# A transformer layer's feed-forward product transposed through VectorE and a DRAM scratch instead of on TensorE

## The chip, the cores and the metric

The kernel runs on one core of a Trainium2 chip. The metric is the device time of one launch in microseconds; the number given is the median of several executions. Beside it there is one execution with the hardware profiler on, from which every row below is taken.

## What is computed

One decoder layer on 256 tokens with 1024 features, all in float32. The part around the change is the SwiGLU feed-forward between two normalizations; the attention before it and the gated input after it are not touched.

```python
f = rmsnorm(h, g_ffn[i])
h = h + (jax.nn.silu(f @ w_gate[i]) * (f @ w_up[i])) @ w_down[i]     # D_FF = 2816
u = rmsnorm(h, g_ple[i])
h = h + jax.nn.sigmoid(u @ w_ple_gate[i]) * (p[i] @ w_ple_proj[i])
return rmsnorm(h, g_final)
```

## The kernel before

**Precision.** Each float32 matmul is three matmuls of TensorE's reduced type `F32R` (`mm3`, lines 174 to 177). A weight chunk is loaded as `raw`, ScalarE copies it rounded to `hi` (line 131), VectorE subtracts to get `lo` (line 158), and TensorE sums hi x H, lo x H and hi x L, where H and L are the same two parts of the activations.

**Weights.** They come in chunks of 1024 KB on SP's queue in the order of the table `CHUNKS`. `raw`, `hi` and `lo` have three buffers each; `need` starts loads three chunks ahead. A load waits until the split three chunks earlier has read its buffer; a cast to `hi` waits until TensorE is done with the chunk three earlier.

**Feed-forward.** The 2816 columns go in blocks (`FF_BLOCKS`): five of 512 and one of 256. For each block `b` the gate weights (`j` = 0) and the up weights (`j` = 1) are two chunks each, of four k-slices; for each of the two row tiles `t` (128 tokens) TensorE makes one accumulation group of 24 matmuls, `ff{b}{t}{j}`. Block 5 has gate and up side by side in one group. The order is b, j, t, k. So of a pair of chunks the first is used in the first half of both row tiles' groups, and the second in the second halves; the second one's buffer, taken over from the first of the pair before, comes free late and is wanted soon.

**The product.** When the gate group ends ScalarE takes its silu into `sg`; when the up group ends VectorE multiplies both into `hid` (128 tokens x 512 columns, line 712). The down-projection needs it with the columns on the partitions. `hid_T` (lines 674 to 682) does that one group later: TensorE transposes it in 128x128 squares with the identity into PSUM (`hidt`), ScalarE rounds into `hidH`, VectorE subtracts into `hidL`.

**Down-projection.** Four accumulators (two row tiles x two halves of the 1024 columns) over 22 k-slices, `wd`. The first two k-slices are done accumulator by accumulator, since the last two PSUM buffers are still being read by ScalarE and VectorE for block 5. The last `hid` is transposed after k = 6.

**What sets the order.** TensorE's order is the order of the code. The other engines' order is made by a scheduler from the order of the code, priorities and estimated times; on the chip each engine then works strictly in that order and waits on semaphores. SP issues all the loads, also in order.

Of the kernel before, what the change touches and what calls it, by code (L numbers as in the profile page):

```python
# [8 lines left out]
F32 = mybir.dt.float32  # L9
F32R = mybir.dt.float32r  # L10
BF16 = mybir.dt.bfloat16
I32 = mybir.dt.int32
AF = mybir.ActivationFunctionType
ALU = mybir.AluOpType
AX = mybir.AxisListType

P = 128
D = 1024
# [4 lines left out]
NQ = 512  # L23
# [13 lines left out]
FF_BLOCKS = [(b * NQ, min(NQ, DFF - b * NQ)) for b in range((DFF + NQ - 1) // NQ)]  # L37
# [25 lines left out]
def layer_kernel(  # L63
# [13 lines left out]
    nc = tc.nc  # L77
# [9 lines left out]
    def acc(name):  # L87
        return ps_acc.tile([P, NQ], F32, tag="acc", name=name)

    def aux(name):  # L90
        return ps_aux.tile([P, NQ], F32, tag="aux", name=name)

    chunks, off = [], 0
    for kind, k0, nk, width, _, _ in CHUNKS:
        n = P * nk * width
# [86 lines left out]
    def tsl(t):  # L182
        return slice(t * P, (t + 1) * P)

    def rsqrt(m, n, name):
        y = sm.tile([P, n], F32, tag=f"rs_y{n}", name=f"{name}_y", bufs=6)
        i = sm.tile([P, n], I32, tag=f"rs_i{n}", name=f"{name}_i")
        a = sm.tile([P, n], F32, tag=f"rs_a{n}", name=f"{name}_a")
        h = sm.tile([P, n], F32, tag=f"rs_h{n}", name=f"{name}_h")
        nc.vector.tensor_scalar(i, m.bitcast(I32), 1, None, op0=ALU.arith_shift_right)  # L190
        nc.vector.tensor_scalar(y.bitcast(I32), i, -1.0, float(0x5F3759DF), op0=ALU.mult, op1=ALU.add)
        nc.vector.tensor_scalar(h, m, -0.5, None, op0=ALU.mult)
        for _ in range(3):
            if n == 1:
                nc.vector.scalar_tensor_tensor(a, y, h, y, op0=ALU.mult, op1=ALU.mult)
            else:
                nc.vector.tensor_tensor(a, y, y, op=ALU.mult)
                nc.vector.tensor_tensor(a, a, h, op=ALU.mult)
            nc.vector.scalar_tensor_tensor(y, a, 1.5, y, op0=ALU.add, op1=ALU.mult)
        return y  # L200
# [64 lines left out]
    ident = cst.tile([P, P], F32, tag="ident", name="ident")  # L265
# [5 lines left out]
    with actx:  # L271
        cadd = at.tile([P, 256], F32, tag="cadd", name="cadd")
        init = at.tile([P, 256], F32, tag="init", name="init")
        for tl, fill in ((cadd, BIG), (init, NEG)):
            nc.gpsimd.memset(tl, 0.0)
            nc.gpsimd.affine_select(
                out=tl[:, P:256], in_=tl[:, P:256], pattern=[[-1, P]], compare_op=ALU.is_ge,
# [335 lines left out]
        i = 0  # L613
# [7 lines left out]
    for nm, g in (("ffn", g_ffn), ("ple", g_ple), ("fin", g_fin)):  # L621
        gB[nm] = act.tile([P, D], F32, tag="gB", name=f"gB{nm}", bufs=2)
        nc.sync.dma_start(gB[nm], g.partition_broadcast(P))
    ff = state["ff"] = ctx.enter_context(tc.tile_pool(name="ff", bufs=2))
    hgs = {}

# [34 lines left out]
    def rstd_h(t, name):  # L661
        s1 = sm.tile([P, 1], F32, tag="ss1", name=f"ss_{name}{t}")
        m1 = sm.tile([P, 1], F32, tag="m1", name=f"m_{name}{t}")
        sqt = ff.tile([P, D], BF16, tag="sqt", name=f"sq_{name}{t}", bufs=1)
        nc.scalar.activation(sqt, h[:, t, :], AF.Square, accum_out=s1)
        nc.vector.tensor_scalar(m1, s1, 1.0 / D, EPS, op0=ALU.mult, op1=ALU.add)
        return rsqrt(m1, 1, f"{name}{t}")


    hidH = ff.tile([P, KF, 256], F32R, tag="hidH", name="hidH", bufs=1)  # L670
    hidL = ff.tile([P, KF, 256], F32R, tag="hidL", name="hidL", bufs=1)
    rf = {0: rstd_h(0, "f")}

    def hid_T(b, t, hid, w):
        nb = w // P
        pt = aux(f"hidt{b}{t}")
        for i in range(nb):
            nc.tensor.transpose(pt[:, i * P : (i + 1) * P], hid[:, i * P : (i + 1) * P], ident)  # L678
        pv = pt[:, :w].rearrange("p (b n) -> p b n", b=nb)
        kk = slice(4 * b, 4 * b + nb)  # L680
        nc.scalar.copy(hidH[:, kk, tsl(t)], pv)  # L681
        nc.vector.tensor_tensor(hidL[:, kk, tsl(t)], pv, hidH[:, kk, tsl(t)].bitcast(F32), op=ALU.subtract)  # L682

    pend = []
    for b, (f0, w) in enumerate(FF_BLOCKS):
        pgu = {}
        both = 2 * w <= NQ
        cw = 2 * w if both else w
        for j in range(1 if both else 2):
            for t in range(NT):  # L690
                ps = acc(f"ff{b}{t}{j}")
                for k in range(KD):
                    wH, wL = need(f"f{b}_{j}", k - k % 4)
                    mm3(
                        ps[:, :cw], FH[:, k, tsl(t)], FL[:, k, tsl(t)], wH[:, k % 4, :], wL[:, k % 4, :],
                        k == 0, k == KD - 1,
                    )
                    if (b, j, t) == (0, 0, 0) and k in (4, 7):
                        trn(1, int(k == 7), FH, FL, "f")
                pgu[(j, t)] = ps  # L700
                if b == 0 and (j, t) == (0, 0):
                    rf[1] = rstd_h(1, "f")
                if pend:
                    hid_T(*pend.pop(0))
                if j == 0:
                    sg = ff.tile([P, NQ], F32, tag="sg", name=f"sg{b}{t}", bufs=3)
                    nc.scalar.activation(sg[:, :w], ps[:, :w], AF.Silu, scale=rf[t])  # L707
                    pgu[("s", t)] = sg
                if j == 1 or both:
                    up = ps[:, cw - w : cw]  # L710
                    hid = ff.tile([P, NQ], F32, tag="hid", name=f"hid{b}{t}", bufs=3)
                    nc.vector.scalar_tensor_tensor(  # L712
                        hid[:, :w], up, rf[t], pgu[("s", t)][:, :w], op0=ALU.mult, op1=ALU.mult
                    )
                    pend.append((b, t, hid, w))

    pd = {(t, c): acc(f"wd{t}{c}") for t in range(NT) for c in range(2)}
    TAILK = KF - 4
# [10 lines left out]
    for k in range(2, TAILK):  # L729
        for t in range(NT):  # L730
            for c in range(2):
                wd_mms(k, t, c)
        if k == 6:
            hid_T(*pend.pop(0))
    UH = act.tile([P, KD, 256], F32R, tag="XH", name="UH")
    UL = act.tile([P, KD, 256], F32R, tag="XL", name="UL")
    for t in range(NT):
        for c in range(2):
# [5 lines left out]
            if (t, c) == (1, 0):  # L744
                trn(0, 0, UH, UL, "u")
    ru = {0: rstd_h(0, "u")}


# [10 lines left out]
    def ple_evac(t, f0, w, ps, prev, mid=None):  # L759
        cc = slice(f0, f0 + w)  # L760
        sg = ff.tile([P, NQ], F32, tag="sg", name=f"sgp{t}{f0}", bufs=3)
        nc.scalar.activation(sg[:, :w], ps[:, :w], AF.Sigmoid, scale=ru[t])
        nc.vector.tensor_tensor(sg[:, :w], sg[:, :w], pp[:, t, cc], op=ALU.mult)
        nc.vector.tensor_tensor(h[:, t, cc], h[:, t, cc], sg[:, :w], op=ALU.add)
        sqt = ff.tile([P, NQ], F32, tag="hid", name=f"sq_o{t}{f0}", bufs=3)
        s3 = sm.tile([P, 1], F32, tag="s3", name=f"s3{t}{f0}")
        if prev is None and t == 0:
            nc.scalar.activation(sqt[:, :w], h[:, t, cc], AF.Square, accum_out=s3)
        else:
            nc.vector.tensor_tensor_reduce(  # L770
                sqt[:, :w], h[:, t, cc], h[:, t, cc], 1.0, 0.0 if prev is None else prev, ALU.mult, ALU.add, s3
            )
        if mid:
            mid()
        if t == 0:
            nc.gpsimd.tensor_tensor(h[:, t, cc], h[:, t, cc], gB["fin"][:, cc], op=ALU.mult)
        else:
            nc.vector.tensor_tensor(h[:, t, cc], h[:, t, cc], gB["fin"][:, cc], op=ALU.mult)
        return s3
# [17 lines left out]
    with tc.manual_schedule(engines={mybir.EngineType.PE, mybir.EngineType.Activation, mybir.EngineType.DVE}):  # L797

        m = sm.tile([P, 1], F32, tag="m3", name="m30")
# [39 lines left out]
def _pack(inputs):  # L839
    import numpy as np  # L840

    a = {k: np.asarray(v) for k, v in inputs.items()}

    def rows(w):
        return np.ascontiguousarray(w.reshape(-1, P, w.shape[-1]).transpose(1, 0, 2))

    xT = a["x"][0].T.reshape(KD, P, 256)
    gT = a["g_attn"][0].reshape(KD, P, 1)
    w0 = a["w_in"][0][:, IN_GROUPS[0][0] : IN_GROUPS[0][1]].reshape(KD, P, W0)
    def cols(names, r0, r1, c0, width):  # L850
        names = names if isinstance(names, tuple) else (names,)
        n = width // len(names)
        return np.concatenate([a[name][0][r0:r1, c0 : c0 + n] for name in names], axis=1)

    flat = [rows(cols(name, k0 * P, (k0 + nk) * P, c0, width)).ravel() for _, k0, nk, width, name, c0 in CHUNKS]
    return {
        "xa": np.ascontiguousarray(np.concatenate([gT, xT, w0], axis=2)).ravel(),
        "x": rows(a["x"][0]),
        "pT": rows(np.ascontiguousarray(a["p"][0, 0].T)).reshape(P, -1),
        "w": np.concatenate(flat),  # L860
        "g_k": a["g_idx_k"][0],
        "g_ffn": a["g_ffn"][0],
        "g_ple": a["g_ple"][0],
        "g_fin": a["g_final"],
        "cs": _tables(),
    }
# [23 lines left out]
```

## Time and profile before

| | us |
|---|---|
| median of 3 runs | 335.91 (335.6 to 335.98) |
| the profiled execution | 335.19 |
| its span, first to last instruction | 333.4 |
| TensorE (PE) busy | 324.3, 97% of the span |
| VectorE (DVE) busy | 227.0, 68% |
| ScalarE (ACT) busy | 175.2, 53% |

Of the chain of work that ended last, 81% of the span is TensorE's, 12% VectorE's, 4% ScalarE's. The feed-forward groups run from about 116 to 240 us, the down-projection from 240 to about 306. In a timeline row the first number is the start in us from the span's start, the second the length; for a matmul the end is modelled and overlaps the next one, so that only the distance of starts tells what it costs. Square brackets give how long the engine had been idle and what released it.

### The profile page before, as it was taken

What the parts mean: (1) busy time and instruction counts of PE and PEld (TensorE: products, weight loads), DVE (VectorE), ACT (ScalarE), POOL (GpSimd) and SP (SyncE); (2) the same over time, 40 slices, a digit from 0 to 9 for tenths busy, and PEclk for the clock granted to TensorE, in tenths of its full rate; (3) what the DMA queues carried; (4) which work ended last, traced back from release to release, by engine and by line L of the source; (5) the groups of instructions that cost most, each with busy time, mean ns of one, the idle gap of its engine ahead of it and who ended that gap; (6) DMA issues with size and microseconds to landing.
All of it is one profiled execution on the core that took longest, in us unless ns stands there. A gap on an engine that the chain in (4) does not pass through costs nothing.

```text
span 333.4 us, 4350 instructions
## 1 busy us (share of the span) xinstructions
PE 324.3 (97%) x1637; PEld 264.4 (79%) x1637; DVE 227.0 (68%) x464; ACT 175.2 (53%) x278; POOL 5.6 (2%) x16
## 2 busy tenths in 40 slices
PE   8999999999999999999999999999999999999992
PEld 8888887677677888888888888888878888888891
DVE  4969999999996886634753655367462535379884
ACT  5957355986674574533562455335443424238623
POOL 2001000000000000000000000000000000000110
PEclk9999999999999999999999999999999999999997
DMA  7996938410337076357435634563365555550002
GB/s 267 418 372 241 362 129 323 141 43 2 126 126 255 0 265 229 134 193 253 158 112 237 252 124 143 239 230 132 144 252 178 201 165 213 161 216 3 0 34 94
DMA packets 10389, 59.71 MB, mean 179 GB/s; under 512 B 1280, under 2 KB 1536, under 8 KB 4096
## 3 DMA queue, kind: packets, MB, share of 16 engines
q1 hardware_dynamic: 10224, 59.24, 48.8%
q8 instruction: 13, 0.21, 0.3%
q10 hardware_dynamic: 144, 0.20, 0.2%
q14 instruction: 8, 0.07, 0.1%
HBM read 58.38 MB, written 1.05 MB: 178 GB/s over the span
## 4 chain that ended last, share of the span: by engine, by line
PE 81%; DVE 12%; ACT 4%; issue 1%; ACTq 0%
PE g L312 13%; PE ff L175 12%; PE ff L177 12%; PE ff L176 12%; PE wd L175 6%; PE wd L176 6%; PE wd L177 6%; DVE lo L158 3%; PE pg L177 2%; PE pg L175 2%; PE pg L176 2%; ACT hi L131 2%; PE hidt L678 1%; DVE score L429 1%; DVE m L428 1%
## 5 line engine op out<-in xcount | busy, mean ns | idle before, releaser
L158 DVE TENSOR_TENSOR lo<-raw,hi 128x1024 fp32r<-128x1024 f32 (+1 forms) x99 | 116.5, 1208 | 62.7 <-ACT hi L131 62.6
L131 ACT CAST hi<-raw 128x1024 fp32r<-128x1024 f32 (+1 forms) x99 | 98.5, 1041 | 91.7 <-PE ff L177 42.4
L175 PE MATMUL ff<-hi,FH 128*128 128x512 f32 x176 | 69.6, 396 | 0.0
L177 PE MATMUL ff<-hi,FL 128*128 128x512 f32 x176 | 68.6, 390 | 0.0
L176 PE MATMUL ff<-lo,FH 128*128 128x512 f32 x176 | 68.5, 389 | 0.0
L177 PEld LDWEIGHTS ff<-hi,FL 128*128 128x128 f32 x176 | 33.0, 188 | 7.0
L176 PEld LDWEIGHTS ff<-lo,FH 128*128 128x128 f32 x176 | 33.1, 188 | 6.5
L175 PEld LDWEIGHTS ff<-hi,FH 128*128 128x128 f32 x176 | 33.1, 188 | 6.5
L175 PE MATMUL wd<-hi,hidH 128*128 128x512 f32 x88 | 35.2, 400 | 0.0
L176 PE MATMUL wd<-lo,hidH 128*128 128x512 f32 x88 | 34.9, 397 | 0.0
L177 PE MATMUL wd<-hi,hidL 128*128 128x512 f32 x88 | 34.6, 393 | 0.0
L312 PE MATMUL g<-hi,XH 128*128 128x512 f32 x64 | 25.8, 408 | 0.0
L312 PE MATMUL g<-hi,XL 128*128 128x512 f32 x64 | 24.8, 393 | 0.0
L312 PE MATMUL g<-lo,XH 128*128 128x512 f32 x56 | 21.6, 391 | 0.0
L175 PEld LDWEIGHTS wd<-hi,hidH 128*128 128x128 f32 x88 | 16.5, 188 | 4.2 <-issue 0.3
L177 PEld LDWEIGHTS wd<-hi,hidL 128*128 128x128 f32 x88 | 16.5, 188 | 4.1
L176 PEld LDWEIGHTS wd<-lo,hidH 128*128 128x128 f32 x88 | 16.5, 188 | 3.6
L707 ACT ACTIVATE sg<-ff,f_y 128x512 f32<-128x512 f32 (+1 forms) x12 | 7.8, 649 | 17.3 <-PE ff L177 17.3
L712 DVE SCALAR_TENSOR_TENSOR hid<-ff,f_y,sg 128x512 f32<-128x512 f32 (+1 forms) x12 | 8.4, 703 | 12.1 <-PE ff L177 10.0
L682 DVE TENSOR_TENSOR hidL<-hidt,hidH 128x512 fp32r<-128x512 f32 (+1 forms) x12 | 7.7, 643 | 11.4 <-ACT hidH L681 11.3
L312 PEld LDWEIGHTS g<-hi,XH 128*128 128x128 f32 x64 | 12.0, 188 | 3.0 <-issue 0.7
L312 PEld LDWEIGHTS g<-hi,XL 128*128 128x128 f32 x64 | 12.0, 188 | 2.7
(201 smaller groups left out, 453.7 us busy)
## 6 DMA issues: line engine op xcount, KB each, us to landing
raw<-in_w_dram SPq DMA_DIRECT2D x48, 1024.0 KB, 4.9
a<-in_xa_dram SPq DMA_DIRECT2D x8, 354.5 KB, 5.8
raw_g<-in_w_dram SPq DMA_DIRECT2D x2, 512.0 KB, 7.7
h<-in_x_dram SPq DMA_DIRECT2D x1, 1024.0 KB, 11.2
raw<-in_w_dram SPq DMA_DIRECT2D x2, 256.0 KB, 4.1
raw<-in_w_dram SPq DMA_DIRECT2D x1, 512.0 KB, 8.3
gBffn<-in_g_ffn_dram SPq DMA_DIRECT2D x1, 512.0 KB, 5.9
gBple<-in_g_ple_dram SPq DMA_DIRECT2D x1, 512.0 KB, 5.9
```

Source lines behind the costliest of these rows:

```text
L131: nc.scalar.copy(hi[:, o : o + step], raw[:, o : o + step])
L158: nc.vector.tensor_tensor(lo[:, o:e], raw[:, o:e], hi[:, o:e].bitcast(F32), op=ALU.subtract)
L175: nc.tensor.matmul(ps, aH, wH, start=start, stop=False)
L176: nc.tensor.matmul(ps, aH, wL, start=False, stop=False)
L177: nc.tensor.matmul(ps, aL, wH, start=False, stop=stop)
L312: nc.tensor.matmul(pss[t][:, :width], aT[:, k, tsl(t)], wT, start=k == 0 and n == 0, stop=k == KD - 1 and n == 2,)
L428: nc.vector.max(m8, s[:, :n])
L429: nc.vector.match_replace(s[:, :n], m8, s[:, :n], SENT)
L678: nc.tensor.transpose(pt[:, i * P : (i + 1) * P], hid[:, i * P : (i + 1) * P], ident)
L682: nc.vector.tensor_tensor(hidL[:, kk, tsl(t)], pv, hidH[:, kk, tsl(t)].bitcast(F32), op=ALU.subtract)
L707: nc.scalar.activation(sg[:, :w], ps[:, :w], AF.Silu, scale=rf[t])
L712: nc.vector.scalar_tensor_tensor(hid[:, :w], up, rf[t], pgu[("s", t)][:, :w], op0=ALU.mult, op1=ALU.mult)
```

## The change

`hid_T` goes, and with it every transpose of the product on TensorE. In its place stand three steps. `hid_out`: VectorE transposes `hid` in 32x32 blocks into `hidb`, and one transfer writes that to a scratch tile in DRAM, `hidd`. `hid_in`: four transfers bring it back, each to 32 partitions of `hidt`, in pieces of 128 columns (512 bytes; 256 in block 5). `hid_split`: ScalarE and VectorE make `hidH` and `hidL` as before, now from SBUF. `hid_step` staggers them: at each new product the split of the one two before, the way back of the one before and the way out of the new one are put into the program; two more steps stand in the down-projection after k = 2 and k = 6. The rows of `w_down` are permuted on the host to fit. The squares of `rstd_h` use the `sg` buffers, and `hid` has two buffers instead of three.

```diff
+    def hid_out(b, t, hid, w):
+        tb = ff.tile([P, NQ], F32, tag="hidB", name=f"hidb{b}{t}", bufs=2)
+        nc.vector.transpose(tb[:, :w], hid[:, :w])
+        dr = dram.tile([P, NQ], F32, tag="hidD", name=f"hidd{b}{t}")
+        nc.sync.dma_start(dr[:, :w], tb[:, :w])
+        return b, t, w, dr
+
+    def hid_in(b, t, w, dr):
+        ht = ff.tile([P, NQ], F32, tag="hidt", name=f"hidt{b}{t}", bufs=2)
+        n = w // 4
+        for g in range(4):
+            nc.sync.dma_start(
+                ht[32 * g : 32 * g + 32, :w].rearrange("p (s n) -> p s n", s=4),
+                dr[:, g * n : g * n + n].rearrange("(s j) n -> j s n", s=4),
+            )
+        return b, t, w, ht
+
+    def hid_split(b, t, w, ht):
         nb = w // P
-        pt = aux(f"hidt{b}{t}")
-        for i in range(nb):
-            nc.tensor.transpose(pt[:, i * P : (i + 1) * P], hid[:, i * P : (i + 1) * P], ident)
-        pv = pt[:, :w].rearrange("p (b n) -> p b n", b=nb)
+        pv = ht[:, :w].rearrange("p (s b i) -> p b s i", s=4, b=nb)
         kk = slice(4 * b, 4 * b + nb)
-        nc.scalar.copy(hidH[:, kk, tsl(t)], pv)
-        nc.vector.tensor_tensor(hidL[:, kk, tsl(t)], pv, hidH[:, kk, tsl(t)].bitcast(F32), op=ALU.subtract)
...
+    def hid_step(*new):
+        if hq["in"]:
+            hid_split(*hq["in"].pop(0))
+        if hq["out"]:
+            hq["in"].append(hid_in(*hq["out"].pop(0)))
+        if new:
+            hq["out"].append(hid_out(*new))
...
-                if pend:
-                    hid_T(*pend.pop(0))
...
-                    pend.append((b, t, hid, w))
+                    hid_step(b, t, hid, w)
...
-        if k == 6:
-            hid_T(*pend.pop(0))
+        if k in (2, 6):
+            hid_step()
```

TensorE's order at the turn from block 0 to block 1 (`ff011` is block 0, row tile 1, up; `ff100` block 1, row tile 0, gate), before and then changed:

```order
L175 MATMUL ff011_1475<-hi19_1333,FH_1258 128x512
L176 MATMUL ff011_1475<-lo19_1458,FH_1258 128x512
L177 MATMUL ff011_1475<-hi19_1333,FL_1259 128x512
L678 MATMUL hidt00_1500<-ident_229,hid00_1473 128x128 x4
L175 MATMUL ff100_1509<-hi20_1353,FH_1258 128x512
L176 MATMUL ff100_1509<-lo20_1515,FH_1258 128x512
```

```order
L175 MATMUL ff011_1481<-hi19_1335,FH_1260 128x512
L176 MATMUL ff011_1481<-lo19_1460,FH_1260 128x512
L177 MATMUL ff011_1481<-hi19_1335,FL_1261 128x512
L175 MATMUL ff100_1517<-hi20_1355,FH_1260 128x512
L176 MATMUL ff100_1517<-lo20_1523,FH_1260 128x512
```

The four transposes of the product of block 0, row tile 0, are gone; the groups now stand directly behind each other. The same holds at eleven more places.

ScalarE's order around the products of block 1 (`hidt10`, `hidt11`) and the casts of chunks 26 to 29, of which the odd ones are the second of their pair, before and then changed:

```order
L131 CAST hi26_1609<-raw26_1607 128x1024 x2
L681 CAST hidH_1310<-hidt10_1654 128x4x128
L707 ACTIVATE sg20_1711<-ff200_1663,f0_y_1317 128x512
L681 CAST hidH_1310<-hidt11_1704 128x4x128
L131 CAST hi27_1666<-raw27_1664 128x1024 x2
L131 CAST hi28_1686<-raw28_1684 128x1024 x2
L707 ACTIVATE sg21_1738<-ff210_1713,f1_y_1390 128x512
L131 CAST hi29_1743<-raw29_1741 128x1024 x2
```

```order
L131 CAST hi26_1610<-raw26_1608 128x1024 x2
L700 CAST hidH_1312<-hidt10_1670 128x4x128
L735 ACTIVATE sg20_1720<-ff200_1679,f0_y_1319 128x512
L131 CAST hi27_1682<-raw27_1680 128x1024 x2
L131 CAST hi28_1702<-raw28_1700 128x1024 x2
L735 ACTIVATE sg21_1747<-ff210_1722,f1_y_1392 128x512
L700 CAST hidH_1312<-hidt11_1794 128x4x128
L131 CAST hi29_1752<-raw29_1750 128x1024 x2
```

The copy of row tile 0 keeps its place, ahead of the cast of chunk 27; that of row tile 1 moves three places on, to directly ahead of the cast of chunk 29.

SP's order over the same stretch (`raw` are weight loads, `hidd` the way out to DRAM, `hidt` the four transfers back), before and then changed:

```order
L120 DMA raw28_1684<-in_w_dram 128x2048
L120 DMA raw29_1741<-in_w_dram 128x2048
L120 DMA raw30_1761<-in_w_dram 128x2048
L120 DMA raw31_1818<-in_w_dram 128x2048
```

```order
L682 DMA hidd10_1639<-hidb10_1637 128x512
L689 DMA hidt10_1670<-hidd10_1639 32x4x128 x4
L120 DMA raw28_1700<-in_w_dram 128x2048
L682 DMA hidd11_1677<-hidb11_1675 128x512
L120 DMA raw29_1750<-in_w_dram 128x2048
L689 DMA hidt11_1794<-hidd11_1677 32x4x128 x3
L120 DMA raw30_1770<-in_w_dram 128x2048
L689 DMA hidt11_1794<-hidd11_1677 32x4x128
L120 DMA raw31_1842<-in_w_dram 128x2048
```

Between the loads stand the new transfers; the last of the four for row tile 1 stands behind the load of chunk 30.

## Rows read from the trace of the kernel before

**Rows 1.** Stretch; its length; busy PE, PEld, DVE, ACT, POOL; clock, DMA share, GB/s:
```profile
138.00:225.00 87.00, 87.00 (x401) 72.16 (x400) 46.73 (x47) 38.98 (x46) 0.00 (x0) 1.00 0.53 191
```
**Rows 2.** TensorE's timeline (start, length) at a turn with no transposes:
```profile
154.93 0.39 PE L177 MATMUL ff<-hi,FL 128*128 128x512 f32 x1
...
155.38 0.39 PE L176 MATMUL ff<-lo,FH 128*128 128x512 f32 x1
```
**Rows 3.** TensorE's timeline at a turn with four transposes:
```profile
160.37 0.39 PE L177 MATMUL ff<-hi,FL 128*128 128x512 f32 x1
160.60 0.60 PE L678 MATMUL hidt<-ident,hid 128*128 128x128 f32 x4
160.95 0.48 PE L175 MATMUL ff<-hi,FH 128*128 128x512 f32 x1
161.27 0.39 PE L176 MATMUL ff<-lo,FH 128*128 128x512 f32 x1
```
**Rows 4.** All instructions on the tile hidt: count, shortest, median, longest ns:
```profile
L678 PE MATMUL hidt<-ident,hid x44: 270/271/273, 137.9 to 260.5; 128*128 128x128 f32 x44
```
**Rows 5.** TensorE's timeline at the turn with two transposes:
```profile
240.21 0.39 PE L177 MATMUL ff<-hi,FL 128*128 128x512 f32 x1
...
240.89 0.40 PE L176 MATMUL wd<-lo,hidH 128*128 128x512 f32 x1
```
**Rows 6.** TensorE's timeline where the fourth down-projection accumulator begins:
```profile
244.64 0.40 PE L177 MATMUL wd<-hi,hidL 128*128 128x512 f32 x1
244.96 0.48 PE L175 MATMUL wd<-hi,hidH 128*128 128x512 f32 x1
245.27 0.39 PE L176 MATMUL wd<-lo,hidH 128*128 128x512 f32 x1
```
**Rows 7.** VectorE's timeline, around block 1 and at the turn into the down-projection:
```profile
155.36 0.75 DVE L712 SCALAR_TENSOR_TENSOR hid<-ff,f_y,sg 128x512 f32<-128x512 f32 x1 [2.00 <-PE ff L177]
159.16 2.36 DVE L158 TENSOR_TENSOR lo<-raw,hi 128x1024 fp32r<-128x1024 f32 x2 [3.06 <-ACT hi L131]
161.44 0.74 DVE L712 SCALAR_TENSOR_TENSOR hid<-ff,f_y,sg 128x512 f32<-128x512 f32 x1
162.10 2.35 DVE L158 TENSOR_TENSOR lo<-raw,hi 128x1024 fp32r<-128x1024 f32 x2
164.37 0.68 DVE L682 TENSOR_TENSOR hidL<-hidt,hidH 128x512 fp32r<-128x512 f32 x1
...
241.72 2.36 DVE L158 TENSOR_TENSOR lo<-raw,hi 128x1024 fp32r<-128x1024 f32 x2 [0.36 <-ACT hi L131]
244.00 0.42 DVE L682 TENSOR_TENSOR hidL<-hidt,hidH 128x256 fp32r<-128x256 f32 x1
244.34 0.47 DVE L712 SCALAR_TENSOR_TENSOR hid<-ff,f_y,sg 128x256 f32<-128x256 f32 x1
```
**Rows 8.** ScalarE's timeline, the same stretches:
```profile
158.07 2.01 ACT L131 CAST hi<-raw 128x1024 fp32r<-128x1024 f32 x2 [5.58 <-PE ff L177]
...
162.70 0.57 ACT L681 CAST hidH<-hidt 128x512 fp32r<-128x512 f32 x1
...
169.87 2.01 ACT L131 CAST hi<-raw 128x1024 fp32r<-128x1024 f32 x2 [2.01 <-PE ff L177]
...
180.75 2.01 ACT L131 CAST hi<-raw 128x1024 fp32r<-128x1024 f32 x2 [5.57 <-PE ff L177]
...
240.64 2.00 ACT L131 CAST hi<-raw 128x1024 fp32r<-128x1024 f32 x2 [0.72 <-PE ff L177]
```
**Rows 9.** SP's timeline of DMA issues, four from 161.55, and the third alone:
```profile
161.55 14.85 SPq L120 DMA_DIRECT2D raw<-in_w_dram  x4
...
173.35 0.33 SPq L120 DMA_DIRECT2D raw<-in_w_dram  x1
```
**Rows 10.** DMA issues: count, KB each, median us from issue to landing:
```profile
raw<-in_w_dram SPq DMA_DIRECT2D x48, 1024.0 KB, 4.9
...
out_dram<-h SPq DMA_DIRECT2D x2, 256.0 KB, 3.2
...
gk<-in_g_k_dram SPq DMA_DIRECT2D x1, 32.0 KB, 11.3
```

More of the change, by code (lines that the diff above doesn't have):

```diff
@@ L623, in layer_kernel @@
         nc.sync.dma_start(gB[nm], g.partition_broadcast(P))
+    dram = ctx.enter_context(tc.tile_pool(name="dram", bufs=3, space=bass.MemoryType.DRAM))
     ff = state["ff"] = ctx.enter_context(tc.tile_pool(name="ff", bufs=2))
@@ L663, in rstd_h @@
         m1 = sm.tile([P, 1], F32, tag="m1", name=f"m_{name}{t}")
-        sqt = ff.tile([P, D], BF16, tag="sqt", name=f"sq_{name}{t}", bufs=1)
+        sqt = ff.tile([P, D], BF16, tag="sg", name=f"sq_{name}{t}", bufs=3)
         nc.scalar.activation(sqt, h[:, t, :], AF.Square, accum_out=s1)
@@ L672, in layer_kernel @@
     rf = {0: rstd_h(0, "f")}
-    def hid_T(b, t, hid, w):
+    def hid_out(b, t, hid, w):
[14 more added lines that the diff above has]
+    def hid_split(b, t, w, ht):
         nb = w // P
-        pt = aux(f"hidt{b}{t}")
-        for i in range(nb):
-            nc.tensor.transpose(pt[:, i * P : (i + 1) * P], hid[:, i * P : (i + 1) * P], ident)
-        pv = pt[:, :w].rearrange("p (b n) -> p b n", b=nb)
+        pv = ht[:, :w].rearrange("p (s b i) -> p b s i", s=4, b=nb)
         kk = slice(4 * b, 4 * b + nb)
-        nc.scalar.copy(hidH[:, kk, tsl(t)], pv)
-        nc.vector.tensor_tensor(hidL[:, kk, tsl(t)], pv, hidH[:, kk, tsl(t)].bitcast(F32), op=ALU.subtract)
-    pend = []
+        hH = hidH[:, kk, tsl(t)].rearrange("p b (s i) -> p b s i", s=4)
+        nc.scalar.copy(hH, pv)
+        nc.vector.tensor_tensor(
+            hidL[:, kk, tsl(t)].rearrange("p b (s i) -> p b s i", s=4), pv, hH.bitcast(F32), op=ALU.subtract
+        )
+    hq = {"out": [], "in": []}
+    def hid_step(*new):
[5 more added lines that the diff above has]
+            hq["out"].append(hid_out(*new))
     for b, (f0, w) in enumerate(FF_BLOCKS):
@@ L710, in layer_kernel @@
                     up = ps[:, cw - w : cw]
-                    hid = ff.tile([P, NQ], F32, tag="hid", name=f"hid{b}{t}", bufs=3)
+                    hid = ff.tile([P, NQ], F32, tag="hid", name=f"hid{b}{t}", bufs=2)
                     nc.vector.scalar_tensor_tensor(
@@ L764, in ple_evac @@
         nc.vector.tensor_tensor(h[:, t, cc], h[:, t, cc], sg[:, :w], op=ALU.add)
-        sqt = ff.tile([P, NQ], F32, tag="hid", name=f"sq_o{t}{f0}", bufs=3)
+        sqt = ff.tile([P, NQ], F32, tag="hid", name=f"sq_o{t}{f0}", bufs=2)
         s3 = sm.tile([P, 1], F32, tag="s3", name=f"s3{t}{f0}")
@@ L853, in cols, with down @@
         return np.concatenate([a[name][0][r0:r1, c0 : c0 + n] for name in names], axis=1)
+    def down(m):
+        parts = [m[f0 : f0 + n].reshape(4, n // P, 32, -1).transpose(1, 0, 2, 3).reshape(n, -1) for f0, n in FF_BLOCKS]
+        return np.concatenate(parts, axis=0)[None]
+    a["w_down"] = down(a["w_down"][0])
     flat = [rows(cols(name, k0 * P, (k0 + nk) * P, c0, width)).ravel() for _, k0, nk, width, name, c0 in CHUNKS]
```

## The prediction

> **What bounds the kernel now.** I read the table of stretches first. From 138 to 225 us TensorE is busy for all of 87.00 us, VectorE for 46.73, ScalarE for 38.98, the DMA engines for 0.53 of the time, and the granted clock is 1.00, the 2.4 GHz level [rows 1]. So in the feed-forward stage whatever TensorE issues is time, and the other engines have room for about as much again. Then I read TensorE's own timeline, by starts and not by busy time, because the ends are modelled. At a turn of one accumulation group to the next with nothing between, the start of L177's last matmul and that of the next group's L176 lie 155.38 - 154.93 = 0.45 us apart, two steps of 0.227 [rows 2]. At a turn with four transposes of the product the same two starts lie 161.27 - 160.37 = 0.90 apart [rows 3]. Four transposes thus cost 0.45 us of TensorE's stream, 0.11 each, although a single record lasts 0.27 [rows 4]: that is depth of the pipeline and not occupancy.
>
> **What is removed.** The 44 transposes are ten groups of four and two groups of two (blocks 0 to 4 are 512 wide, block 5 is 256). All ten turns read alike in the timeline: 10 x 0.45 = 4.5 us. The first group of two gives 240.89 - 240.21 = 0.68 against two plain steps of 0.23, so 0.22, and the second (in the down-projection after k = 6) the same [rows 5]. Together 4.95 us.
>
> What is late next? After each turn TensorE goes straight on to matmuls whose weights are already split. One small stall can go as well: L177 at 244.64 is followed by 244.96 and 245.27, steps of 0.32 and 0.31 where 0.23 is the rule, 0.17 us in all [rows 6]. There the fourth down-projection accumulator waits for a PSUM buffer that VectorE's `hid` of block 5, row tile 1, is the last to read (it starts at 244.34 and takes 0.47). Ahead of it VectorE did a `hidL` of 0.42 [rows 7] and the two halves of a weight split, released by a cast that began at 240.64 [rows 8]. In the changed order that `hidL` (block 5, row tile 0) is no longer between the split and `hid`; the product would be ready at about 244.08 + 0.47 = 244.55, before TensorE needs it at 244.64 + 0.23 = 244.87. I take 0.17 for it; bounds 0 and 0.17.
>
> **What is added, and what covers it.** VectorE gets twelve block transposes. No such operation is in the trace; the nearest is `hidL` with 0.68 us for the same 128x512, and the bound above I take as a whole pair of split halves, 2.36 [rows 7]; below, 0. I take 0.7, so 8 us in over 100 us, on an engine that idles 40 us of 87. Its place matters more than its sum: for row tile 0 it stands directly behind `hid`, for row tile 1 between the two halves of the next split.
>
> SP gets 60 transfers. Weight loads are issued four in 14.85 us, in pairs [rows 9], so SP has time to spare; 60 issues at the 0.33 us of a single one are 20 us over the stage, hidden by SP's own waiting. They move 2816 KB out and 2816 KB back. A full block of the feed-forward reads four loads of 1024 KB [rows 10] and would get 1024 KB more, so at equal efficiency the share of 0.53 becomes 0.66. If the 512-byte pieces of the way back moved at a quarter of the rate of the loads (191 GB/s at a share of 0.53, so 360 at full share, 0.73 us for 256 KB and 2.9 at a quarter), a block of 22 us would hold 2 x 3.6 = 7.3 us more, share 0.86. Both bounds stay under 1, and I book nothing.
>
> The real price can only come through waits in order. ScalarE's copy `hidH` now waits for a transfer, and behind it in ScalarE's order stand weight casts; behind its subtraction on VectorE stand weight splits. Only the cast of a group's second chunk is tight. Take the one at 158.07, released by TensorE's last use of the buffer: its split starts at 159.16, the first half is ready at 160.34 [rows 7, 8], and TensorE first wants that half with the fourteenth matmul of the group that starts at 160.95, at 161.27 + 12 x 0.227 = 163.99 [rows 3]. That is 3.6 us of slack, 3.2 once the transposes in between are gone. Such a cast stands behind a copy in seven places: row tile 0 of blocks 0 to 3, row tile 1 of blocks 0 to 2.
>
> Row tile 0: `hid` of block 1 ends at 156.11 [rows 7], the transpose at about 156.8. The next tight cast behind its copy starts at 169.87; two groups of transposes less make that 168.97, and the copy of 0.57 must precede it [rows 8]: 168.4. So the round trip may take 11.6 us without any loss, 14.8 with the slack. Its rows: 256 KB to DRAM took 3.2 us from issue to landing, a whole 1024 KB load 4.9 [rows 10]; together 8.1. As an upper end for the way back I take the worst small load, 32 KB that landed after 11.3 us behind a queue of large ones [rows 10]: 14.5, still inside.
>
> Row tile 1: `hid` ends at 162.18, half a split follows until 163.3, the transpose until 164.0. Out by 167.2. Three of the four transfers back follow at once, but the fourth stands in SP's order behind the next weight load, whose issue falls at 173.35 [rows 9]. Behind that load's 4.9 us it lands near 178.6. The tight cast stands at 180.75 [rows 8], the copy must start at 180.2; both are less by the same 0.9. Margin 1.6, with the slack 4.8. Block 2 has two parts behind a load in the same way. This is the tightest place, and by the rows nothing is lost there.
>
> Weight loads behind a waiting transfer on SP: the load issued at 173.35 lands at 178.25, and its cast stands behind the one that runs from 180.75 to 182.76, so 4.5 us of waiting cost nothing. In the down-projection the buffers turn once in 5.6 us (24 matmuls of 0.23), with three of them, and the two last copies have still wider room: their columns are wanted only at the end of that stage. The other edits (the squares sharing the `sg` buffers, two `hid` buffers for three) add no instruction and their last readers are a whole group old: 0.
>
> **Two rules of the Trainium skill.** The page "VectorE: DVE Perf Modes" (The three transpose paths) gives 390 ns for a 128x128 transpose on TensorE. By it the 44 would be worth an estimated 17.2 us; the trace's spacing says 0.11 us each, and I go by the trace. The same section, and "DMA: Bandwidth & Descriptors" (Rules for kernel authors), call a plain DMA with a rearranged pattern 19 times slower than the transposing one; by it a read-back of 256 KB would be an estimated 13.9 us and the queues would be the bound, time well over 400 us. No run here shows such a transfer yet; its pieces here are whole runs of 512 bytes. It speaks for the slow rival below.
>
> **The sum.** The profiled execution took 335.19 us (span 333.4). Less 4.95, less 0.17: 330.07. It was 0.72 below the median of the runs, 335.91, so for the median 335.91 - 5.12 = 330.8. I predict 330.8, with its own range 330.2 (the copies save a little more) to 331.8 (a few waits of some tenths).
>
> **Rivals.**
> A, partly paid back. The late parts of the read-back in blocks 1 and 2, or the `hid` at the turn into the down-projection (0.3 us of margin, each us late is a us of TensorE), overrun by 1 to 1.5 us each: 332 to 334.5, say 333. For: the margin of 1.6 is the smallest of all. Against: the cast's slack of 3.2 comes on top.
> B, slower: ScalarE in its order waits for the read-back at the seven tight casts. It costs from a round trip of 14.8 us on, and decides the sign when the excess adds up to 5.1 us, at about 16.1 us on the four places of row tile 0. At 18 us it is 4 x 3.2 = 12.8 us, so 335.91 - 5.12 + 12.8 = 343.6. For: no small-piece read-back from DRAM, and no wait of one transfer for another, is in the trace; the loads come in bursts. Against: the rows make 8.1.
> C, no change: the 5 us come back through A in several blocks at once, or TensorE's steps grow by 1% under the added traffic. Against: with the DMA engines at a share of 0.53 the step already is the plain 0.227.
> D, more gained, toward the page's price: each transpose also holds up the matmuls around it beyond the turn. 318.7 by 17.2 us. Against: two transposes cost half of what four cost, 0.22 and 0.45, so nothing fixed hangs on a turn.
>
> **Numbers.** Forecast 0.79, A 0.09, B 0.08, C 0.03, D 0.01. Within 0.2% (0.7 us) is about what a measurement of this kernel can't tell from no change. Faster takes the forecast, A and D: 0.89; same 0.03; slower 0.08. The range reaches from 330.0 to 333.5, forecast and most of A.
>
> **What would show it.** After: no TensorE instruction writes `hidt`; at the turns L177 to the next L176 0.45 us; down-projection about 4.5 us earlier; no TensorE step over 0.4 us between 138 and 300; ScalarE's `hidH` waits for a transfer, but the casts of second chunks still start when TensorE releases the buffer. Round trips near 8 us. Wrong: TensorE waiting for a `lo` or `hi` right behind a `hidH` or `hidL`, or SP's loads landing later than their casts are due.

## The result and the profile after

The changed kernel takes 331.06 us (330.69 to 331.42) against 335.79 before: ratio 0.9859, 95% interval 0.9842 to 0.9876. Predicted were 330.8, range 330.0 to 333.5. The profiled execution has a span of 329.6 us.

The same stretch of the feed-forward, in the table of stretches (length, busy time and instructions of PE, PEld, DVE, ACT, POOL, then clock, DMA share, GB/s):

```profile
138.00:225.00 87.00, 87.00 (x385) 72.09 (x384) 52.62 (x56) 41.08 (x48) 0.00 (x0) 1.00 0.69 242
```

TensorE is as full as in [rows 1], with 385 instructions for 401. VectorE has gone from 46.73 to 52.62 us, the DMA share from 0.53 to 0.69. TensorE's timeline at the turn that [rows 3] showed, from block 1 to block 2:

```profile
160.43 0.39 PE L177 MATMUL ff<-hi,FL 128*128 128x512 f32 x1
160.65 0.39 PE L175 MATMUL ff<-hi,FH 128*128 128x512 f32 x1
160.88 0.39 PE L176 MATMUL ff<-lo,FH 128*128 128x512 f32 x1
```

L177 to L176 is now 0.45 us, as in [rows 2], where it was 0.90. From the first matmul of the feed-forward to the first of the gate after the down-projection (`pg`) TensorE's timeline of before has

```profile
115.18 0.40 PE L175 MATMUL ff<-hi,FH 128*128 128x512 f32 x1
...
303.53 0.40 PE L175 MATMUL pg<-hi,UH 128*128 128x512 f32 x1
```

that is 303.53 - 115.18 = 188.35 us, and the timeline of the changed kernel

```profile
116.16 0.40 PE L175 MATMUL ff<-hi,FH 128*128 128x512 f32 x1
...
299.44 0.40 PE L175 MATMUL pg<-hi,UH 128*128 128x512 f32 x1
```

that is 183.28: 5.07 less, where the prediction's sum had 4.95 and 0.17, together 5.12. But the stretch begins 0.98 us later than in the profile of before, so that the spans differ by 3.8 only. That part of the program is unchanged; the experiments come back to it.

The new instructions, from the views of the tiles `hidb` and `hidt` (shortest, median, longest ns; first and last start) and of the DMA issues (count, KB each, median us to landing):

```profile
L680 DVE STREAM_TRANSPOSE hidb<-hid x12: 445/706/712, 134.4 to 241.0; 128x512 f32<-128x512 f32 x10, 128x256 f32<-128x256 f32 x2
```
```profile
L689 SPq DMA_DIRECT2D hidt<-hidd x48: 303/430/676, 137.3 to 247.0; - x48
```
```profile
raw<-in_w_dram SPq DMA_DIRECT2D x48, 1024.0 KB, 5.1
...
hidd<-hidb SPq DMA_DIRECT2D x10, 256.0 KB, 2.8
hidt<-hidd SPq DMA_DIRECT2D x40, 64.0 KB, 4.2
```

The block transpose takes 0.71 us, close to the `hidL` of [rows 7]. An issue of the way back holds SP for 0.43 us in the median, not the 0.33 of [rows 9]: the first of the four takes 0.33 or less where SP stood before it, like a load, and the three directly behind another issue mostly take 0.42 to 0.43. The weight loads land in 5.1 us, before in 4.9 [rows 10].

SP's timeline around the products of block 1, where `hidd` is the way out and `hidt` the way back:

```profile
156.94 0.33 SPq L682 DMA_DIRECT2D hidd<-hidb  x1
160.22 1.75 SPq L689 DMA_DIRECT2D hidt<-hidd  x4
162.07 0.38 SPq L120 DMA_DIRECT2D raw<-in_w_dram  x1
164.02 0.34 SPq L682 DMA_DIRECT2D hidd<-hidb  x1
165.13 0.33 SPq L120 DMA_DIRECT2D raw<-in_w_dram  x1
167.86 1.27 SPq L689 DMA_DIRECT2D hidt<-hidd  x3
172.49 0.35 SPq L120 DMA_DIRECT2D raw<-in_w_dram  x1
172.88 0.43 SPq L689 DMA_DIRECT2D hidt<-hidd  x1
```

and ScalarE's timeline, in which these copies stand, with block 2 (square brackets: idle time before it and its releaser):

```profile
163.57 0.62 ACT L700 CAST hidH<-hidt 128x512 fp32r<-128x512 f32 x1 [0.70 <-DMA hidt<-hidd]
...
177.78 0.62 ACT L700 CAST hidH<-hidt 128x512 fp32r<-128x512 f32 x1 [3.46 <-DMA hidt<-hidd]
179.89 2.01 ACT L131 CAST hi<-raw 128x1024 fp32r<-128x1024 f32 x2 [1.49 <-PE ff L177]
...
200.14 0.62 ACT L700 CAST hidH<-hidt 128x512 fp32r<-128x512 f32 x1 [4.07 <-DMA hidt<-hidd]
201.65 2.01 ACT L131 CAST hi<-raw 128x1024 fp32r<-128x1024 f32 x2 [0.89 <-PE ff L177]
```

Row tile 0 of block 1: 163.57 - 156.94 = 6.6 us from the issue of the way out to the copy. Row tile 1: the fourth transfer is issued at 172.88 behind a weight load, and the copy starts at 177.78. ScalarE does wait for transfers, 8.2 us in three waits (0.70, 3.46 and 4.07), but each time its next instruction then still waits for TensorE: 2.11 us for the end of a group after the first, 1.49 and 0.89 us for the buffer of the tight cast after the others. Those waits cost nothing, since a second one stands behind them.

The one place where TensorE loses time between 125 and 290 us is the fourth accumulator of the down-projection, as in [rows 6]: in its timeline a step of 0.27 and one of 0.34 where 0.23 is the rule.

```profile
240.79 0.39 PE L177 MATMUL wd<-hi,hidL 128*128 128x512 f32 x1
241.06 0.50 PE L175 MATMUL wd<-hi,hidH 128*128 128x512 f32 x1
241.40 0.39 PE L176 MATMUL wd<-lo,hidH 128*128 128x512 f32 x1
```

What waits there is a weight load of TensorE (PEld), the instruction that brings one operand of the next matmul into the engine. Its timeline at the same place:

```profile
240.56 0.19 PEld L177 LDWEIGHTS wd<-hi,hidL 128*128 128x128 f32 x1
241.06 0.19 PEld L175 LDWEIGHTS wd<-hi,hidH 128*128 128x128 f32 x1 [0.31 <-DVE hid L740]
```

The load at 240.56 belongs to the matmul at 240.79, one step behind it. The next load would have its turn at 240.79 and starts only at 241.06, when `hid` is there.

ScalarE's timeline ahead of it, with the cast that TensorE releases, and VectorE's, with a `hidL`, the weight split and the `hid` that is waited for:

```profile
236.20 0.62 ACT L700 CAST hidH<-hidt 128x512 fp32r<-128x512 f32 x1
237.02 2.01 ACT L131 CAST hi<-raw 128x1024 fp32r<-128x1024 f32 x2 [0.20 <-PE ff L177]
```

```profile
237.66 0.68 DVE L701 TENSOR_TENSOR hidL<-hidt,hidH 128x512 fp32r<-128x512 f32 x1
238.26 2.35 DVE L158 TENSOR_TENSOR lo<-raw,hi 128x1024 fp32r<-128x1024 f32 x2
240.53 0.47 DVE L740 SCALAR_TENSOR_TENSOR hid<-ff,f_y,sg 128x256 f32<-128x256 f32 x1
```

### The profile page after: what moved, and what is told of

The parts are those of the page before. It is cut to its first block, busy times and chain, and to the rows that moved or that the text cites. A ratio compares the mean times of both kernels' runs of the same rounds, so it can differ in the third digit from the quotient of the medians.

```text
span 329.6 us, 4401 instructions
## 1 busy us (share of the span) xinstructions
PE 320.2 (97%) x1593; PEld 260.9 (79%) x1593; DVE 233.9 (71%) x476; ACT 175.8 (53%) x278; POOL 5.6 (2%) x16
## 4 chain that ended last, share of the span: by engine, by line
PE 66%; DVE 18%; ACT 4%; issue 2%; ACTq 0%; DVEq 0%
PE ff L175 12%; PE ff L176 12%; PE ff L177 12%; PE wd L177 6%; PE wd L176 6%; PE wd L175 6%; DVE lo L158 5%; PE pg L177 2%; PE pg L175 2%; PE pg L176 2%; ACT hi L131 2%; DVE score L429 1%; DVE m L428 1%; DVE pr_a L477 1%; DVE pr_b L477 1%
## 5 line engine op out<-in xcount | busy, mean ns | idle before, releaser
L175 PE MATMUL ff<-hi,FH 128*128 128x512 f32 x176 | 68.7, 390 | 0.0
L177 PE MATMUL ff<-hi,FL 128*128 128x512 f32 x176 | 68.5, 389 | 0.0
L176 PE MATMUL ff<-lo,FH 128*128 128x512 f32 x176 | 68.5, 389 | 0.0
L177 PEld LDWEIGHTS ff<-hi,FL 128*128 128x128 f32 x176 | 33.0, 188 | 7.0
L176 PEld LDWEIGHTS ff<-lo,FH 128*128 128x128 f32 x176 | 33.0, 188 | 6.7
L177 PE MATMUL wd<-hi,hidL 128*128 128x512 f32 x88 | 35.1, 398 | 0.0
L176 PE MATMUL wd<-lo,hidH 128*128 128x512 f32 x88 | 34.7, 394 | 0.0
L176 PEld LDWEIGHTS wd<-lo,hidH 128*128 128x128 f32 x88 | 16.5, 188 | 4.2
L177 PEld LDWEIGHTS wd<-hi,hidL 128*128 128x128 f32 x88 | 16.5, 188 | 3.8
L175 PE MATMUL pg<-hi,UH 128*128 128x512 f32 (+1 forms) x40 | 14.1, 352 | 0.0
```

Source lines behind the costliest of these rows:

```text
L175: nc.tensor.matmul(ps, aH, wH, start=start, stop=False)
L176: nc.tensor.matmul(ps, aH, wL, start=False, stop=False)
L177: nc.tensor.matmul(ps, aL, wH, start=False, stop=stop)
```

## Experiments

Kernels of one group ran on one chip beside the kernel before: the transposes put back, the kernel without transposition, the changed kernel again and the turn (before: 335.89 us), then the last four (335.77). The changed kernel itself ran in the first group only, the kernel before once more by itself on a third chip. The stretch is always that from the first feed-forward matmul to the first gate matmul behind the down-projection; the end is counted from the start of the last gate matmul.

**The transposes back on TensorE, everything else as changed.**

```diff
+    def dead_T(b, t, hid, w):
+        pt = aux(f"dead{b}{t}")
+        for i in range(w // P):
+            nc.tensor.transpose(pt[:, i * P : (i + 1) * P], hid[:, i * P : (i + 1) * P], ident)
...
+                if pend:
+                    dead_T(*pend.pop(0))
...
+        if k == 6:
+            dead_T(*pend.pop(0))
...
```

> The changed kernel with the 44 transposes on TensorE put back at their old places, their results unused. Theory: 44 x 0.11 = 4.95 us come back, 336.0. Rival (what was gained was the PSUM reading, the copies' waits or the order of the other engines, and TensorE had room): it stays below 333.

336.79 us, ratio to before 1.0028 (1.0018 to 1.0039). TensorE's timeline at the same turn:

```profile
161.13 0.39 PE L177 MATMUL ff<-hi,FL 128*128 128x512 f32 x1
161.36 0.60 PE L711 MATMUL dead<-ident,hid 128*128 128x128 f32 x4
161.71 0.48 PE L175 MATMUL ff<-hi,FH 128*128 128x512 f32 x1
162.03 0.39 PE L176 MATMUL ff<-lo,FH 128*128 128x512 f32 x1
```

0.90 us again. For the stretch the same timeline has

```profile
115.94 0.40 PE L175 MATMUL ff<-hi,FH 128*128 128x512 f32 x1
...
304.12 0.40 PE L175 MATMUL pg<-hi,UH 128*128 128x512 f32 x1
```

that is 188.18 us, 4.90 more than in the changed kernel; the stall at the fourth accumulator is gone (no step over 0.24 there), so the transposes took 4.90 + 0.14 = 5.04. The rival is refuted: with the new path in place the old transposes cost what they cost before. Of the whole difference of 5.87 us to the changed kernel on this chip, about 1 us lies outside the stretch, most of it in the end (8.06 us against 7.21), where the last two output transfers landed after 3.3 and 3.5 us instead of 2.3 and 2.7. Why they did is open.

**No transposition at all.**

```diff
     def hid_out(b, t, hid, w):
-        tb = ff.tile([P, NQ], F32, tag="hidB", name=f"hidb{b}{t}", bufs=2)
-        nc.vector.transpose(tb[:, :w], hid[:, :w])
...
-        return b, t, w, dr
+        return b, t, w, hid
...
     def hid_in(b, t, w, dr):
-        ht = ff.tile([P, NQ], F32, tag="hidt", name=f"hidt{b}{t}", bufs=2)
...
-        return b, t, w, ht
+        return b, t, w, dr
...
-                    hid = ff.tile([P, NQ], F32, tag="hid", name=f"hid{b}{t}", bufs=2)
+                    hid = ff.tile([P, NQ], F32, tag="hid", name=f"hid{b}{t}", bufs=4)
...
```

> The product is not transposed at all (its rounding and subtraction read it as it stands, so the down-projection gets wrong columns); no block transpose, no scratch, no transfers. Theory (the gain is the stream time of 44 transposes on TensorE, and the way through DRAM is fully covered): the same as the changed kernel within 0.3 us, 331.0, and from the first feed-forward matmul to the first gate matmul after the down-projection 183.2 us. Rival (the waits for the read-back and its traffic cost some tenths each): faster than the changed kernel by 0.5 to 2 us.

330.77 us, ratio to before 0.985 (0.9837 to 0.9862); the changed kernel on the same chip 330.92, 0.9855 (0.984 to 0.9869). TensorE's timeline:

```profile
115.88 0.40 PE L175 MATMUL ff<-hi,FH 128*128 128x512 f32 x1
...
299.05 0.40 PE L175 MATMUL pg<-hi,UH 128*128 128x512 f32 x1
```

The stretch is 183.17 us, 0.11 below the changed kernel; 0.09 of that is the stall at the fourth accumulator, 0.05 here instead of 0.14. So the whole way over VectorE, DRAM and back costs about 0.1 us of the stretch, nearly all of it at that one place. The end is 0.27 us shorter as well, 6.93 for 7.20, to which the sum below comes back. Hardly more is to be had from this step.

**The changed kernel and the kernel before, again.**

> The changed kernel once more. Both theories: 331.1 us. What it tells apart is the front: in the first profile the feed-forward began at 116.16 us against 115.18 before, though no instruction ahead of it changed. If that is chance of the first loads, the begin lies anywhere from 115.0 to 116.3 here; if the DRAM scratch causes it, it is again at 116.0 or later.

Its time and ratio stand above. The feed-forward begins at 115.66, and the stretch is again 183.28.

> The kernel before, profiled again. Where its feed-forward begins and how long its stretch from the first feed-forward to the first gate matmul is. If the begin is chance of the first loads it falls between 115.2 and 116.2 us as in the changed kernels; if the changed kernels are slower there for a reason, again at 115.2. Stretch 188.35 us in both cases.

> The same once more: begin of the feed-forward between 115.2 and 116.2 us by chance, or 115.2 again if the front is faster in this kernel; stretch 188.35 us.

335.61 and 335.71 us; feed-forward from 115.59 and from 115.70, stretch 188.34 both times. Over all profiles the changed kernel and its relatives begin it between 115.32 and 116.22, and the kernel without any scratch (the one above) at 115.88. So the scratch is not the cause. Nor are the first loads, as I had supposed: in the first profile of either kernel TensorE starts its first real matmuls at 4.43 us, and up to the seventh no wait is recorded, but the seventh starts at 5.90 in the kernel before and at 6.82 in the changed one, which is 0.92 of the 0.98. From the second matmul on the changed kernel's steps are 0.36 to 0.38 us where the other's are 0.20 to 0.21, and the trace's record of the granted clock begins, with 1.00 (2.4 GHz), at 6.80 there and at 4.79 in the kernel before. In the other profiles it begins anywhere from 3.63 to 6.98 us, in the kernel before itself at 4.79, 5.65 and 3.63. The later it begins, the later the feed-forward, except in the two profiles with 3.63 and 3.71, where a wait of 0.9 us for a cast takes its place, and in the kernel with one hop more, which loses another 0.34 us ahead of the feed-forward. So the moment at which TensorE's clock rises differs from run to run, also of one kernel, and it moves everything behind it by up to 1 us; what sets it is open.

**The turn into the down-projection.**

```diff
-    for t, c in ((0, 0), (0, 1), (1, 0), (1, 1)):
-        for k in range(2):
-            wd_mms(k, t, c)
-    for k in range(2, TAILK):
+    for k0 in (0, 2):
+        for c in range(2):
+            for k in (k0, k0 + 1):
+                wd_mms(k, 0, c)
+    for c in range(2):
+        for k in range(4):
+            wd_mms(k, 1, c)
+    hid_step()
+    for k in range(4, TAILK):
...
-        if k in (2, 6):
+        if k == 6:
             hid_step()
```

> The changed kernel, with the first two down-projection accumulators taking four k-slices before the last two begin. Theory: only the stall of 0.14 us at the fourth accumulator goes, 330.9, not to be told from the changed kernel by time; the profile has no TensorE step above 0.24 us from 125 to 290 us. Rival (the second down-projection chunk, now wanted 2.8 us after the turn, comes late): a new step of 0.5 us or more near 239 us and no gain.

331.16 us, ratio 0.9854 (0.9839 to 0.9869), not to be told from 330.92. No TensorE step over 0.24 us from 125 to 290; stretch 183.14, that is 0.14 less. As expected, and too small to show in the time.

**The three steps at once, and the way back late.**

First all three at the new product:

```diff
-        if hq["in"]:
-            hid_split(*hq["in"].pop(0))
-        if hq["out"]:
-            hq["in"].append(hid_in(*hq["out"].pop(0)))
         if new:
-            hq["out"].append(hid_out(*new))
+            hid_split(*hid_in(*hid_out(*new)))
```

Then the way back in the step of the split:

```diff
         if hq["in"]:
-            hid_split(*hq["in"].pop(0))
+            hid_split(*hid_in(*hq["in"].pop(0)))
         if hq["out"]:
-            hq["in"].append(hid_in(*hq["out"].pop(0)))
+            hq["in"].append(hq["out"].pop(0))
```

> The changed kernel with all three steps (out, back, split) written at the new product instead of one per product. The scheduler leaves ScalarE's order as it was up to one or two places. Theory (order and waits are set by the estimated arrival, and each lies inside the slack): 331.1 within 0.4 us. Rival (the stagger is what hides the round trip): each of seven tight casts late by one us or more, 335 or above.

> The changed kernel with the way back written only in the step of the split. The copies of both row tiles of blocks 1 and 2 now stand one behind the other directly ahead of one tight cast. Theory: the way back lands about 6 us after the product that triggers it, the copy ends within the 3.2 us of slack behind the release of the buffer: 331.0 to 332. Rival (slower by waits in order): 1 to 2 us lost at each of three casts, 334 to 337.

331.75 us (ratio 0.9883, 0.9868 to 0.9897) and 331.45 (0.9873, 0.9859 to 0.9888). The stretches are 183.29 both times, and TensorE has no new step in either. The changed kernel did not run on this chip; beside its times on the other two, 330.92 and 331.06, they are 0.4 to 0.8 us slower; the intervals of the ratios still overlap, for the first just so. That difference is not in the part that they change. In the profile of the first the end takes 8.12 us (7.20 in the changed kernel), because the last output transfers land 0.9 us later; in the profile of the second it takes 7.73 with the transfers landing as before. Why is open. The stagger in the code hides nothing by itself: ScalarE's waits for the way back are 0.7 us in the first, 9.2 in the second and 8.2 in the changed kernel, and none of them costs TensorE a step that the changed kernel does not have. In the late variant the two copies of block 1 stand one behind the other, at 174.04 and 177.78, and the tight cast behind them still starts 63.73 us after the feed-forward's begin (179.71 - 115.98), as in the changed kernel (179.89 - 116.16).

**One hop more.**

```diff
         nc.sync.dma_start(dr[:, :w], tb[:, :w])
-        return b, t, w, dr
+        d2 = dram.tile([P, NQ], F32, tag="hidD2", name=f"hide{b}{t}")
+        nc.sync.dma_start(d2[:, :w], dr[:, :w])
+        return b, t, w, d2
```

> The changed kernel with one more copy of the product from DRAM to DRAM between out and back: half as much traffic again and a round trip of about 9 us instead of 6.5. Theory: still inside 11.6 us and the engines' share stays under 0.9, so 331.1 within 0.5. Rival (TensorE pays for added traffic or for waits): 332 to 335.

331.5 us (ratio 0.9875, 0.9858 to 0.9891); stretch 183.74. No TensorE step grew in the feed-forward, at a DMA share of 0.81 from 138 to 225 us. The 0.46 us more are one stall, at the turn. TensorE's timeline:

```profile
240.25 0.39 PE L177 MATMUL wd<-hi,hidL 128*128 128x512 f32 x1
240.97 0.51 PE L175 MATMUL wd<-hi,hidH 128*128 128x512 f32 x1 [0.34 <-DVE hid L742]
241.32 0.40 PE L176 MATMUL wd<-lo,hidH 128*128 128x512 f32 x1
```

and VectorE's:

```profile
239.84 0.68 DVE L703 TENSOR_TENSOR hidL<-hidt,hidH 128x512 fp32r<-128x512 f32 x1
240.44 0.48 DVE L742 SCALAR_TENSOR_TENSOR hid<-ff,f_y,sg 128x256 f32<-128x256 f32 x1
```

The `hidL` of block 4, row tile 0, has moved to directly before the `hid` that TensorE waits for, and its 0.68 us become a stall of 0.60 (0.72 + 0.34 for two steps of 0.23). ScalarE's copy ahead of it, at 238.38, starts without a wait: it is the order made by the scheduler that costs here, not late data. This is rival A at the place it was expected, for the price of one instruction.

**The way back three times over.**

```diff
-        for g in range(4):
+        for g in [3, 2, 1, 0] * 2 + [0, 1, 2, 3]:
```

> The changed kernel with each of the four transfers back issued three times, the same bytes over again: twelve issues of 0.43 us on SP and a way back of about 8 us. The scheduler also moves copies and casts. Theory: the first real cost of the read-back: tight casts stand behind a silu that ends with the group, 0.3 us late in each of three or four blocks, and some waits beyond the slack: 332 to 335. Rival 1 (everything stays covered): 331.1. Rival 2 (SP's queue holds up the weight loads): above 340.

357.79 us, ratio 1.0678 (1.0623 to 1.0734). SP's timeline:

```profile
150.79 9.82 SPq L689 DMA_DIRECT2D hidt<-hidd  x12
...
164.51 8.84 SPq L689 DMA_DIRECT2D hidt<-hidd  x12
...
175.78 11.75 SPq L689 DMA_DIRECT2D hidt<-hidd  x12
```

The repeated transfers write where earlier ones may still write, so SP waits for their landing, 47.6 us in 20 waits, and a product holds the queue for 9 to 12 us instead of 1.75. The waits of the engines (total us, times, longest):

```profile
ACT hi L131 <- DMA raw<-in_w_dram: 30.5, 17, 4.1
...
ACT hidH L700 <- DMA hidt<-hidd: 15.8, 7, 3.7
...
PEld ff L176 <- DVE lo L158: 11.1, 6, 2.9
```

and one of TensorE's stalls:

```profile
182.37 0.39 PE L175 MATMUL ff<-hi,FH 128*128 128x512 f32 x1
185.23 0.50 PE L176 MATMUL ff<-lo,FH 128*128 128x512 f32 x1 [2.47 <-DVE lo L158]
```

The weight casts wait for weight loads issued late: 30.5 us, where the changed kernel has 1.9. Of the 26.4 us that the stretch grows (to 209.68), an estimated 5.6 are not waiting: 28 steps between the stalls are 0.427 instead of 0.227 us. I had expected 332 to 335 and missed by 23 us: I counted issues and landings of the repeats, and not that SP waits between them. It is the second rival of that run, and it shows the price of rival B's side: not through the copies' own waits, but through SP's queue, which carries the weights too.

## Why the prediction was right

**TensorE's stream sets the stretch.** Right: the stretch lost 5.07 us with the 44 transposes taken away, 0.03 of it in the stall at the turn, and put back they took 5.04.

**0.11 us per transpose, read from the distance of starts.** Right by a narrow miss: 4.95 worked out, about 5.04 measured. The transposes' records lasted 0.27 [rows 4], which would have made 11.9. The page "VectorE: DVE Perf Modes" of the Trainium skill (The three transpose paths) has 390 ns, for bf16, which the prediction took for an estimated 17.2 us; with 5.04 us for 44 this case gives 0.115 us each, so as a price in a full stream the measurement decides against it.

**The stall of 0.17 at the turn.** Failed in size: it is 0.14 now, only 0.03 went. The prediction gave `hid` 0.32 us of room by removing the `hidL` of block 5, counted to the start of the matmul that needs the buffer. The rows show the wait one step earlier, at that matmul's weight load (240.79, not 241.02); this takes 0.23 from the room, and 0.08 comes back because VectorE's next instruction starts that much before the recorded end of the split (in [rows 7], 244.00 for 244.08). Of the 0.17 that remain two things ate more than all. The two transposes at 240.44 in the kernel before themselves stood between the release of the cast and the need, 0.22 us that went with them. And another `hidL`, of block 4, now stands before the split (237.66) and delays it from 1.08 us after the cast's start to 1.24. So `hid` ends at 241.00, 0.21 after the weight load's turn, and TensorE loses 0.14. The 0.3 us of margin that rival A named at this place were not there.

**VectorE and the queues' shares.** Right: 0.71 us per block transpose for 0.7; the share of 0.69 lies near the lower bound worked out, 0.66, not at 0.86. In this kernel the 512-byte pieces move about as well as their bytes count: from 191 to 242 GB/s the rate rose by 27%, the share by 30%. 64 KB land in a median of 4.2 us, and the transfer issued at 160.22, with every earlier load landed, in 1.9. The 19-fold price that the Trainium skill gives a rearranged plain transfer beside the hardware's own transposing one ("DMA: Bandwidth & Descriptors", Rules for kernel authors) is not seen with runs of this length; the transposing transfer itself did not run here.

**Waits in order.** Right: 6.6 us from way out to copy for row tile 0, with 8.1 reckoned and 11.6 allowed; for row tile 1 a margin of 1.49 where I had 1.6, and 0.89 in block 2. The copies' waits of 8.2 us end before TensorE releases what ScalarE needs next. (24 matmuls of 0.23 are 5.5 us and not the 5.6 of the working; nothing hangs on it.)

**SP.** Low by a third for most issues of the way back (0.43 us directly behind another issue), without effect at 12 products of four; with effect as soon as an issue waits.

**The sum.** 335.91 - 5.12 = 330.8 against 331.06 and 330.92. Medians of the kernel before and after differ by 4.7 and 5.0 us, the stretch by 5.07. Part of the rest is in the end: it takes 6.93 or 6.94 us in three profiles of the kernel before, 7.20 and 7.21 in two of the changed one, with the last output transfers issued and landed alike (2.3 and 2.7 us). Behind the landing SP goes through the semaphores of the transfers in order, about 0.065 us each. In the kernel before that of the last output transfer is checked last, in the changed kernel four more checks stand behind it, 0.26 us; in the kernel with one hop more it is last again. The prediction's sum had no term for the end. The other part is the begin, which moves with the rise of the clock. To the end of the program the change is thus worth 4.8 us and not 5.12, a difference that the range takes up.

## What to carry to other kernels

On a full TensorE price an instruction by how far it pushes the next start, at a turn with it and at one without; its own record includes the pipeline. Work moved off a full engine to engines and queues with room is worth its stream time in full, as here, as long as each new wait ends before another wait that stands behind it in the same order: look for the second wait, and state the margin. When something is removed ahead of a tight wait, its own time leaves the margin too. And count what a matmul waits for from its weight load, one step before it: that is where the wait stood here.

## What the runs showed of the hardware

A block transpose of 128x512 float32 on VectorE took 0.71 us, about as much as a subtraction of that size (0.68). An issue held SP for 0.33 us where SP had stood before it, whether a plain load or the first of the four transfers back, and for 0.38 (the load at 162.07) to 0.43 directly behind another issue. A write to DRAM and a dependent read of it, 256 KB each way with the waits in SP's queue, took 6.6 us from first issue to the copy with no load between, and 13.8 where the fourth transfer stood behind a weight load (164.02 to 177.78). In the kernel with the repeated way back TensorE stood in five steps of 2.39 us or more. Behind the first, at 182.37, its steps were 0.23 us again from the second on; behind the other four they were 0.427 for five to eight matmuls on end. Its table of stretches (columns as above) has there

```profile
272.00:275.50 3.50, 3.50 (x9) 2.73 (x9) 1.17 (x2) 0.40 (x1) 0.00 (x0) 0.50 0.59 126
```

a granted clock of 0.50, the 1.2 GHz level, behind steps of 3.80 and 1.26 us; in the kernels without such stalls it is 1.00 through the feed-forward.
